# Weight products of 256 columns in place of 512 in a two-layer decoder trunk

## The chip, the core and the metric

The kernel runs on one core of one Trainium2 chip. The metric is the device time of one execution in microseconds (us), as the median of several executions. The profiled execution, from which every row below comes, is one execution taken by the hardware profiler. Engines are named as in the profile: PE is the matmul side of TensorE and PEld its weight loads, DVE is VectorE, ACT is ScalarE, POOL is GpSimd, SP issues DMAs.

## The reference

256 tokens of width 2048 pass through two residual layers. The first mixes tokens with a gated MLP, the second with an attention whose keys, values and forget gates come from the residual stream after the first layer. Each is followed by a convolutional feed-forward of width 5632. All products of tokens with a weight matrix are fp32.

```python
def reference(x, ...):
    h = x
    # layer 0
    z = gelu(rmsnorm(h, a_norm) @ a_w_in); u, v = split(z)
    h = h + (u * (W_s @ rmsnorm(v) + b_s)) @ a_w_out
    h = h + conv_ffn(rmsnorm(h, f_norm[0]), ...)
    k, v, c = fox_shared_kv(h, kv_norm, w_kvf, b_f, k_norm)
    # layer 1
    q, g = split(rmsnorm(h, b_norm) @ b_w_qg)
    h = h + (forgetting_attention(q, k, v, c) * sigmoid(g)) @ b_w_out
    h = h + conv_ffn(rmsnorm(h, f_norm[1]), ...)
    return rmsnorm(h, final_norm)

def conv_ffn(xn, w_up, conv_w, conv_b, w_down):
    h = xn @ w_up                      # 2048 -> 2 * 5632
    h = causal depthwise conv (width 3) of h, plus conv_b
    gate, val = split(h)
    return (silu(gate) * val) @ w_down # 5632 -> 2048
```

## The kernel before

**Weights.** Every weight matrix is laid out on the host in chunks of 128 partitions x 1024 fp32, 512 KB each, and read once. `Stream` is the planner of the whole program: a list of 785 chunks in a fixed order (the first one in two pieces, which makes 786 loads), all loaded by SP's queue. In step i of `Stream.run` it issues the load of chunk i+6 (into `raw`, four buffers), has chunk i+3 split in two by ACT and DVE (L82 and L83: `whi`, the weight rounded to the fp32r format, and `wlo`, the remainder; four buffers each), and issues the matmuls of chunk i on PE. After each chunk, `advance` lets every pending generator (the evictions and what follows them) run to its next `yield`, so that this work stands in the engines' queues between the chunks.

**Operands.** The tokens too are held in two parts: in an operand tile (`X1`, `ffn_H`, `mlp_X2`, `att_X2`) every feature row kt has 512 columns, of which the first 256 (`:T`, T = 256 tokens) are the rounded value and the last 256 (`T:`) the remainder. A product is the sum of three: weight high x token high, weight high x token low, weight low x token high.

**Feature-major tiles** (`feat_block`) make two output tiles of 128 features x 256 tokens in one PSUM buffer `ps` (128 x 2 x 512 fp32, m = 0, 1, each 512 wide half is one bank; three buffers). The weight is the stationary operand, the tokens stream past it. For each of four rows j and both m, one product with `whi` streams all 512 columns, so the two token parts land side by side in `ps[:, m, :T]` and `ps[:, m, T:]`; one product with `wlo` streams the first 256 and adds to `ps[:, m, :T]`. A chunk is 8 matmuls of 512 and 8 of 256 columns. 656 chunks are of this kind: `up` 352, `down` 176, and 32 each in `a_in_u`, `a_out`, `b_g` and `b_out`. The two side-by-side halves are added at eviction: `scaled_sum` (L299 to L301: ACT copies the second half into `half`, DVE adds it, DVE multiplies with the token scale `rB`), `residual` and `final` (two adds from PSUM to the residual stream `h`).

**The last tile of the program** (`last_block`, `down` of layer 1, p = 7, 11 chunks) is written otherwise: for each m, four `wlo` products, four `whi` products with the second token half and four with the first, all of 256 columns and all into `ps[:, m, :T]`. Its eviction (`final_tile`) follows each m in the last chunk.

**Token-major tiles** (`tok_block`) make 256 tokens x 512 features. Here the tokens are stationary and the weight chunk streams: for each of two rows and two token blocks tb three matmuls of 512 columns (token high x `whi`, token high x `wlo`, token low x `whi`), 12 to a chunk. 128 chunks are of this kind (`a_in_v`, `b_q`, `kvf_k`, `kvf_v`, 32 each). One small chunk, `kvf_f`, is handled by `forget`.

All weight matmuls go through `mm` (L166), which is why they share that line in the profile; the tiles tell them apart.

Of the kernel before, what the change touches and what calls it, by code (L numbers as in the profile page):

```python
# [10 lines left out]
F32 = mybir.dt.float32  # L11
F32R = mybir.dt.float32r
I32 = mybir.dt.int32
AF = mybir.ActivationFunctionType
# [118 lines left out]
def build(ctx, tc, d, out):  # L133
# [31 lines left out]
    def mm(o, a, b, start, stop):  # L165
        nc.tensor.matmul(o, a, b, start=start, stop=stop, skip_group_check=True)  # L166

    def feat_block(src, x, K, done, last=None):


        if last:
            return last_block(src, x, K, done, last)
        box = {}
        n = K // 4
        for c in range(n):
            def mult(hi, lo, c=c):
                if c == 0:
                    box["ps"] = main_ps()
                ps, xx = box["ps"], x()
                parts = (hi, lo) if c < n - 1 else (lo, hi)  # L180
                for i, part in enumerate(parts):
                    for j in range(4):
                        kt = 4 * c + j
                        for m in range(2):
                            w = part[:, j * 256 + m * P:j * 256 + (m + 1) * P]
                            if part is hi:
                                mm(ps[:, m, :], w, xx[:, kt, :], kt == 0, kt == K - 1)
                            else:
                                mm(ps[:, m, :T], w, xx[:, kt, :T], False, False)
                if c == n - 1:  # L190
                    s.start(done(ps))
            s.chunk(src[c], mult)

    def last_block(src, x, K, done, last):
        box = {}
        n = K // 4
        for c in range(n):
            def mult(hi, lo, c=c):
                if c == 0:
                    box["ps"] = main_ps()  # L200
                ps, xx = box["ps"], x()
                for m in range(2):
                    for part, half in ((lo, 0), (hi, 1), (hi, 0)):
                        for j in range(4):
                            kt = 4 * c + j
                            mm(ps[:, m, :T], part[:, j * 256 + m * P:j * 256 + (m + 1) * P],
                               xx[:, kt, half * T:(half + 1) * T], part is lo and kt == 0,
                               half == 0 and part is hi and kt == K - 1)
                    if c == n - 1:
                        last(ps, m)  # L210
                if c == n - 1:
                    s.start(done(ps))
            s.chunk(src[c], mult)

    def tok_block(src, x, done, load=None, prep=None):

        box = {}
        cuts = [(c, 0, 2) for c in range(8)]
        if prep:
            cuts[:1] = [(0, 0, 1), (0, 1, 1)]  # L220
        for c, j0, nj in cuts:
            def mult(hi, lo, c=c, j0=j0, nj=nj):
                kt0 = 2 * c + j0
                if kt0 == 0:
                    box["ps"] = main_ps()
                ps, xx = box["ps"], x()
                for j in range(nj):
                    kt = kt0 + j
                    w = slice(j * 512, (j + 1) * 512)
# [63 lines left out]
            for i in range(2):  # L293
                nc.vector.tensor_tensor(acc, acc, sq[:, i, :], op=OP.add)

    def scaled_sum(ps, a):

        t = small.tile([P, 2, T], F32, name="half", tag="half", bufs=2)
        nc.scalar.activation(t, ps[:, :, T:], AF.Copy)  # L299
        nc.vector.tensor_tensor(a, ps[:, :, :T], t, op=OP.add)  # L300
        nc.vector.tensor_tensor(a, a, rB[:, None, :].to_broadcast([P, 2, T]), op=OP.mult)  # L301

    def residual(p, gain):

        def done(ps):
# [25 lines left out]

    def final(p, gain):

        def done(ps):
            kts = (2 * p, 2 * p + 1)
            if p < 7:
                sq = small.tile([P, 2, T], F32, name="sq", tag="sq", bufs=2)
                for m, kt in enumerate(kts):
                    nc.vector.tensor_tensor(h[:, kt, :], h[:, kt, :], ps[:, m, :T], op=OP.add)
                    nc.vector.tensor_tensor(h[:, kt, :], h[:, kt, :], ps[:, m, T:], op=OP.add)  # L340
                    nc.scalar.activation(sq[:, m, :], h[:, kt, :], AF.Square)
                if p == 0:
                    nc.vector.tensor_tensor(acc, sq[:, 0, :], sq[:, 1, :], op=OP.add)
                else:
                    for i in range(2):
                        nc.vector.tensor_tensor(acc, acc, sq[:, i, :], op=OP.add)
            for kt in kts:
                nc.scalar.activation(h[:, kt, :], h[:, kt, :], AF.Copy, scale=column(gain + kt))
            if p == 5:
                nc.scalar.activation(warm, ones, AF.Sqrt)  # L350
            if p == 7:
                for m in range(2):
                    sum_tokens(tail["sums"], tail["sq"][:, m, :], False, m == 1)
                v = small.tile([P, 2], F32, name="ts_v", tag="ts_v", bufs=2)
                nc.vector.tensor_scalar(v, tail["sums"][:, :2], 1.0 / D, EPS, op0=OP.mult, op1=OP.add)
                t = small.tile([P, 2], F32, name="rs_t", tag="rs_t2", bufs=2)
                nc.scalar.activation(t, v, AF.Sqrt)
                nc.vector.reciprocal(rcol, t)
                newton(rcol, v, t)
                mp = token_rows()  # L360
                for a, b in ((0, 2), (2, 6), (6, 11), (11, 16)):
                    nc.vector.tensor_tensor(h[:, a:b, :], h[:, a:b, :],  # L362
                                            mp[:, None, :T].to_broadcast([P, b - a, T]), op=OP.mult)
                    nc.sync.dma_start(out[:, a:b, :], h[:, a:b, :])
            yield
        return done
# [66 lines left out]
        return done  # L433

    def u_done(p):
        def done(ps):
            X2, vt, wT, bB, _ = mlp_kept()
            u = ph.temp("u", [P, 2, T])
            scaled_sum(ps, u)
            yield  # L440
            nc.scalar.activation(u, u, AF.Gelu)
            mp = misc_ps()
# [20 lines left out]
        return ph.keep("H", [P, KF, 2 * T], F32R)  # L463

    def up_done(l, i):
        def done(ps):
            state["layer"] = l
            H = ffn_h()
            a = ph.temp("a", [P, 2, T])
            scaled_sum(ps, a)  # L470
            yield
            c = ph.temp("c", [P, 2, T])
            for m in range(2):
# [14 lines left out]

    def ffn(l, done):
        for i in range(KF):  # L490
            feat_block(d[f"up{l}"][4 * i:4 * i + 4], lambda: X1, KD, up_done(l, i))
        for p in range(8):
            feat_block(d[f"down{l}"][11 * p:11 * p + 11], ffn_h, KF, done(p), final_tile if l and p == 7 else None)


    def att(key):
# [155 lines left out]
            yield  # L652

    def g_done(p):
        def done(ps):
            X2, o = att("X2"), att("q")
            gg = ph.temp("big", [P, 512], bufs=6).rearrange("p (a b) -> p a b", a=2)
            scaled_sum(ps, gg)
            yield
            while state["done"] < NH or state["gates"] < p:  # L660
                yield
# [112 lines left out]
```

## Time and profile before

| What | Value |
|---|---|
| Time, median of 3 executions | 2244.74 us (2244.12 to 2244.78) |
| The profiled execution's own time | 2244.26 us |
| Its span, first to last instruction | 2242.6 us |
| Matmul records, weight-load records | 12546, 12546 |
| Weight bytes and inputs read from HBM | 417.88 MB |
| ACT busy, DVE busy | 1193.5 us, 1528.5 us |
| Mean granted TensorE clock | 0.998 |

How to read it: the span is what the profiler saw, and 1.7 us of the execution's own time lie around it. Matmuls are pipelined, and their ends in the profile are modelled, so the busy time of one matmul overlaps the next; what a matmul costs in a stream is the distance between starts, which the timeline shows for groups of equal matmuls. A weight load (PEld) is recorded for each matmul and overlaps with the matmul ahead of it.

### The profile page before, as it was taken

The page shows a single profiled execution, that of the slowest core. Times are in us where ns is not written, and L with a number is a line of the kernel's source. Part 1 is how long each engine was busy: PE and PEld are TensorE (multiplying, and loading weights), DVE is VectorE, ACT ScalarE, POOL GpSimd, SP SyncE. Part 2 cuts the span into 40 slices and gives each one's busy share as a digit, 9 for nine tenths or more (in the row PEclk, how much of TensorE's full clock was granted, in tenths as well). Part 3 has the DMA queues.
Part 4 walks back from the last instruction along what each step waited for, and adds up shares of the span by engine and source line. Part 5 has one row for each costly group of instructions (what it writes and reads, how often), then busy time and mean ns, then how long its engine had stood idle before and what let it go on. Part 6 is the DMA issues. An engine that isn't in the chain of part 4 may idle for free.

```text
span 2242.6 us, 32429 instructions
## 1 busy us (share of the span) xinstructions
PE 2228.1 (99%) x12546; PEld 1927.1 (86%) x12546; DVE 1528.5 (68%) x2219; ACT 1193.5 (53%) x1625; POOL 19.2 (1%) x41
## 2 busy tenths in 40 slices
PE   9999999999999999999999999999999999999998
PEld 7888888888888888888788888888888888888887
DVE  6566777777777755557786567677777777765554
ACT  6544455555555544445444666446555555544442
POOL 0000000000000000000000110000000000000000
PEclk9999999999999999999999999999999999999999
DMA  8555555656555555555555555555555555565553
GB/s 299 180 187 173 191 190 191 192 190 189 193 191 188 190 183 191 197 190 177 171 183 188 166 168 179 187 189 193 191 188 188 191 191 191 190 196 188 191 190 127
DMA packets 116443, 422.12 MB, mean 188 GB/s; under 512 B 13232, under 2 KB 13376, under 8 KB 116032
## 3 DMA queue, kind: packets, MB, share of 16 engines
q1 hardware_dynamic: 115344, 417.93, 56.7%
q0 software_dynamic: 768, 2.10, 0.3%
q8 instruction: 98, 1.61, 0.3%
q14 instruction: 57, 0.47, 0.1%
q10 hardware_dynamic: 176, 0.02, 0.0%
HBM read 417.88 MB, written 2.11 MB: 187 GB/s over the span
## 4 chain that ended last, share of the span: by engine, by line
PE 99%; DVE 0%; DMA 0%; ACT 0%; SPq 0%; DVEq 0%; issue 0%
PE ps L166 97%; PE mp L446 0%; PE mp L530 0%; PE mp L616 0%; DMA raw<-a_in_v 0%; PE mp L631 0%; PE mp L639 0%; PE mp L640 0%; PE mp L615 0%; PE mp L638 0%; DVE h L362 0%; PE mp L329 0%; PE mp L277 0%; DVE wlo L83 0%; DVEq L768 0%; ACT whi L82 0%
## 5 line engine op out<-in xcount | busy, mean ns | idle before, releaser
L83 DVE TENSOR_TENSOR wlo<-raw,whi 128x1024 fp32r<-128x1024 f32 (+1 forms) x786 | 953.3, 1221 | 378.8 <-ACT whi L82 377.3
L82 ACT ACTIVATE whi<-raw 128x1024 fp32r<-128x1024 f32 (+1 forms) x786 | 822.1, 1054 | 383.2 <-PE ps L166 353.9
L166 PE MATMUL ps<-X,whi 128*128 128x512 f32 x3328 | 829.6, 396 | 0.0
L166 PEld LDWEIGHTS ps<-X,whi 128*128 128x128 f32 x3328 | 602.7, 188 | 120.4
L166 PEld LDWEIGHTS ps<-X,wlo 128*128 128x128 f32 x3328 | 426.2, 188 | 28.1
L166 PE MATMUL ps<-X,wlo 128*128 128x256 f32 x3328 | 430.7, 277 | 0.0
L166 PE MATMUL ps<-ffn_H,whi 128*128 128x512 f32 (+1 forms) x1496 | 355.4, 381 | 0.0
L166 PEld LDWEIGHTS ps<-ffn_H,whi 128*128 128x128 f32 x1496 | 258.7, 188 | 45.3
L299 ACT ACTIVATE half<-ps 128x512 f32<-128x512 f32 x104 | 62.1, 597 | 256.1 <-PE ps L166 256.1
L166 PEld LDWEIGHTS ps<-ffn_H,wlo 128*128 128x128 f32 x1408 | 184.6, 188 | 13.8 <-DVE h L324 0.3
L166 PE MATMUL ps<-ffn_H,wlo 128*128 128x256 f32 x1408 | 188.5, 277 | 0.2 <-DVE h L324 0.2
L300 DVE TENSOR_TENSOR ffn_a<-ps,half 128x512 f32<-128x512 f32 x88 | 60.9, 692 | 175.1 <-ACT half L299 175.1
L166 PE MATMUL ps<-whi,att_X 128*128 128x512 f32 x512 | 168.1, 400 | 0.0
L480 DVE SCALAR_TENSOR_TENSOR ffn_c<-ffn_a,col,ffn_c 128x255 f32<-128x255 f32 x352 | 162.1, 481 | 6.3
L166 PE MATMUL ps<-whi,X 128*128 128x512 f32 x512 | 162.8, 395 | 0.9 <-ACT whi L82 0.9
L476 ACT ACTIVATE ffn_c<-ffn_a,col 128x256 f32<-128x256 f32 x176 | 96.4, 595 | 47.3 <-DVE ffn_a L301 47.3
L166 PEld LDWEIGHTS ps<-whi,X 128*128 128x128 f32 x512 | 96.2, 188 | 21.9 <-ACT whi L82 1.5
L166 PEld LDWEIGHTS ps<-whi,att_X 128*128 128x128 f32 x512 | 96.3, 188 | 20.4
L166 PE MATMUL ps<-wlo,X 128*128 128x512 f32 x256 | 99.7, 390 | 1.0 <-DVE wlo L83 1.0
L166 PE MATMUL ps<-wlo,att_X 128*128 128x512 f32 x256 | 100.0, 391 | 0.0
L245 ACT ACTIVATE X<-h,col 128x256 fp32r<-128x256 f32 x64 | 29.0, 500 | 101.8 <-DVE h L308 99.5
L250 ACT ACTIVATE ffn_H<-ffn_c 128x256 fp32r<-128x256 f32 x88 | 36.7, 418 | 70.2 <-DVE ffn_c L484 70.2
(147 smaller groups left out, 1215.0 us busy)
## 6 DMA issues: line engine op xcount, KB each, us to landing
raw<-up SPq DMA_DIRECT2D x352, 512.0 KB, 3.8
raw<-down SPq DMA_DIRECT2D x176, 512.0 KB, 4.2
raw<-a_in_u SPq DMA_DIRECT2D x32, 512.0 KB, 3.6
raw<-a_out SPq DMA_DIRECT2D x32, 512.0 KB, 4.3
raw<-b_q SPq DMA_DIRECT2D x32, 512.0 KB, 4.2
raw<-kvf_k SPq DMA_DIRECT2D x32, 512.0 KB, 4.0
raw<-kvf_v SPq DMA_DIRECT2D x32, 512.0 KB, 3.6
raw<-b_g SPq DMA_DIRECT2D x32, 512.0 KB, 3.3
```

The source lines that it names most:

```text
L82: self.nc.scalar.activation(hi[:, :n], raw, AF.Copy)
L83: self.nc.vector.tensor_tensor(lo[:, :n], raw, hi[:, :n].bitcast(F32), op=OP.subtract)
L166: nc.tensor.matmul(o, a, b, start=start, stop=stop, skip_group_check=True)
L245: nc.scalar.activation(dst[:, kt, :T], h[:, kt, :], AF.Copy, scale=g)
L250: nc.scalar.activation(dst[..., :T], src, AF.Copy)
L299: nc.scalar.activation(t, ps[:, :, T:], AF.Copy)
L300: nc.vector.tensor_tensor(a, ps[:, :, :T], t, op=OP.add)
L476: nc.scalar.activation(c[:, m, :], a[:, m, :], AF.Identity, scale=w[2], bias=column(C_CONVB + l * 2 * KF + f))
L480: nc.vector.scalar_tensor_tensor(c[:, m, n:], a[:, m, :T - n], w[k], c[:, m, n:], op0=OP.mult, op1=OP.add)
```

## The change

It has three parts. Line numbers of the code after the change are a few lower than before from `tok_block` on.

1. **Feature-major tiles.** A product of `whi` with 512 token columns becomes two products with the same stationary weight, one per token half, and both add to `ps[:, m, :T]`, where the `wlo` product adds too. A chunk is then 24 matmuls of 256 columns. An argument `wide` names chunks that keep the 512-column product: 66 of 656 (all of `b_g`, 32; one chunk of each `a_in_u` tile, 8; one chunk each in `a_out` and `b_out`; in each layer, the four chunks of the first `up` tile, one chunk of each of six further ones, and one chunk each of two `down` tiles). `last_block` is gone; its tile uses the same code, with m outermost in the last chunk alone. In every chunk the `whi` products now come first; before, the last chunk of a tile had `wlo` first.
2. **Evictions.** A tile without a wide chunk has nothing in `ps[:, m, T:]`. The ACT copy and one DVE add are left out there; `scaled_sum` becomes `scaled`, which multiplies from PSUM. `final` handles both rows of a tile in one instruction.
3. **Token-major tiles.** Each matmul of 512 weight columns becomes two of 256 columns with the same stationary tokens, into the two halves of the same bank.

The products and the sums are the same; the number of weight matmuls in the program goes from 12 152 to 18 320 (6168 more), and a weight load goes with each.

```diff
-    def feat_block(src, x, K, done, last=None):
-        if last:
-            return last_block(src, x, K, done, last)
+    def feat_block(src, x, K, done, wide=(), tile_done=None):
...
-                parts = (hi, lo) if c < n - 1 else (lo, hi)
-                for i, part in enumerate(parts):
+                def product(part, half, j, m):
+                    kt = 4 * c + j
+                    w = part[:, j * 256 + m * P:j * 256 + (m + 1) * P]
+                    first = kt == 0 and part is hi and half in (None, 0)
+                    last = kt == K - 1 and part is lo
+                    if half is None:
+                        mm(ps[:, m, :], w, xx[:, kt, :], first, False)
+                    else:
+                        mm(ps[:, m, :T], w, xx[:, kt, half * T:(half + 1) * T], first, last)
+                halves = (None,) if c in wide else (0, 1)
+                if tile_done and c == n - 1:
+                    for m in range(2):
+                        for j in range(4):
+                            for half in halves:
+                                product(hi, half, j, m)
+                        for j in range(4):
+                            product(lo, 0, j, m)
+                        tile_done(ps, m)
+                else:
                     for j in range(4):
-                        kt = 4 * c + j
                         for m in range(2):
-                            w = part[:, j * 256 + m * P:j * 256 + (m + 1) * P]
-                            if part is hi:
-                                mm(ps[:, m, :], w, xx[:, kt, :], kt == 0, kt == K - 1)
-                            else:
-                                mm(ps[:, m, :T], w, xx[:, kt, :T], False, False)
+                            for half in halves:
+                                product(hi, half, j, m)
+                    for j in range(4):
+                        for m in range(2):
+                            product(lo, 0, j, m)
                 if c == n - 1:
-                    s.start(done(ps))
+                    s.start(done(ps, bool(wide)))
...
-                        mm(ps[:, tb, :], a, hi[:, w], kt == 0, False)
-                        mm(ps[:, tb, :], a, lo[:, w], False, False)
-                        mm(ps[:, tb, :], b, hi[:, w], False, kt == KD - 1)
+                        for i, (st, mv) in enumerate(((a, hi), (a, lo), (b, hi))):
+                            for q in range(2):
+                                mm(ps[:, tb, q * T:(q + 1) * T], st, mv[:, j * 512 + q * T:j * 512 + (q + 1) * T],
+                                   kt == 0 and i == 0 and q == 0, kt == KD - 1 and i == 2)
...
-    def scaled_sum(ps, a):
-        t = small.tile([P, 2, T], F32, name="half", tag="half", bufs=2)
-        nc.scalar.activation(t, ps[:, :, T:], AF.Copy)
-        nc.vector.tensor_tensor(a, ps[:, :, :T], t, op=OP.add)
-        nc.vector.tensor_tensor(a, a, rB[:, None, :].to_broadcast([P, 2, T]), op=OP.mult)
+    def scaled(ps, both, a):
+        src = ps[:, :, :T]
+        if both:
+            nc.scalar.activation(a, ps[:, :, T:], AF.Copy)
+            nc.vector.tensor_tensor(a, ps[:, :, :T], a, op=OP.add)
+            src = a
+        nc.vector.tensor_tensor(a, src, rB[:, None, :].to_broadcast([P, 2, T]), op=OP.mult)
...
-            nc.vector.tensor_tensor(hh, hh, ps[:, :, T:], op=OP.add)
+            if both:
+                nc.vector.tensor_tensor(hh, hh, ps[:, :, T:], op=OP.add)
...
-            feat_block(d[f"up{l}"][4 * i:4 * i + 4], lambda: X1, KD, up_done(l, i))
+            feat_block(d[f"up{l}"][4 * i:4 * i + 4], lambda: X1, KD, up_done(l, i),
+                       range(4) if i == 0 else (0,) if i % 8 == 1 else ())
-            feat_block(d[f"down{l}"][11 * p:11 * p + 11], ffn_h, KF, done(p), final_tile if l and p == 7 else None)
+            feat_block(d[f"down{l}"][11 * p:11 * p + 11], ffn_h, KF, done(p), (0,) if p % 4 == 0 else (),
+                       final_tile if l and p == 7 else None)
...
-        feat_block(d["a_in_u"][4 * p:4 * p + 4], lambda: X1, KD, u_done(p))
+        feat_block(d["a_in_u"][4 * p:4 * p + 4], lambda: X1, KD, u_done(p), (1,) if p else (0,))
-        feat_block(d["a_out"][4 * p:4 * p + 4], mlp_x2, KD, residual(p, C_FNORM))
+        feat_block(d["a_out"][4 * p:4 * p + 4], mlp_x2, KD, residual(p, C_FNORM), () if p else (1,))
-        feat_block(d["b_g"][4 * p:4 * p + 4], lambda: X1, KD, g_done(p))
+        feat_block(d["b_g"][4 * p:4 * p + 4], lambda: X1, KD, g_done(p), range(4))
-        feat_block(d["b_out"][4 * p:4 * p + 4], lambda: att("X2"), KD, residual(p, C_FNORM + KD))
+        feat_block(d["b_out"][4 * p:4 * p + 4], lambda: att("X2"), KD, residual(p, C_FNORM + KD), () if p else (0,))
```

PE's instructions in the `up` stage of layer 0, from the second tile on (`X_73` is `X1`; of the two names behind the arrow the first is streamed and the second stationary; the size is that of the output). Before:

```order
L277 MATMUL mp<-ident,rcol 128x128 x2
L166 MATMUL ps<-X_73,whi 128x512 x8
L166 MATMUL ps<-X_73,wlo 128x256 x8
L166 MATMUL ps<-X_73,whi 128x512 x8
L166 MATMUL ps<-X_73,wlo 128x256 x8
L166 MATMUL ps<-X_73,whi 128x512 x8
```

With the change:

```order
L273 MATMUL mp<-ident,rcol 128x128 x2
L166 MATMUL ps<-X_73,whi 128x512 x8
L166 MATMUL ps<-X_73,wlo 128x256 x8
L166 MATMUL ps<-X_73,whi 128x256 x16
L166 MATMUL ps<-X_73,wlo 128x256 x8
L166 MATMUL ps<-X_73,whi 128x256 x16
```

The second tile's first chunk is one of those that stay wide; from its second chunk on, eight `whi` matmuls of 512 columns have become sixteen of 256, while the `wlo` rows stay as they were.

PE's instructions at the end of the program, in the last chunk of the last tile, where PE waits for DVE's add to `h` between the two m. Before:

```order
L166 MATMUL ps<-ffn_H,wlo 128x256 x4
L166 MATMUL ps<-ffn_H,whi 128x256 x8
L329 MATMUL mp<-ones,acc 128x1 x2
L166 MATMUL ps<-ffn_H,wlo 128x256 x4
L166 MATMUL ps<-ffn_H,whi 128x256 x8
L329 MATMUL mp<-ones,sq 128x1 x4
```

With the change:

```order
L166 MATMUL ps<-ffn_H,whi 128x256 x8
L166 MATMUL ps<-ffn_H,wlo 128x256 x4
L328 MATMUL mp<-ones,acc 128x1 x2
L166 MATMUL ps<-ffn_H,whi 128x256 x8
L166 MATMUL ps<-ffn_H,wlo 128x256 x4
L328 MATMUL mp<-ones,sq 128x1 x4
```

The counts and the place of the two sums are the same; `whi` and `wlo` have changed places.

More of the change, by code (lines that the diff above doesn't have):

```diff
@@ L184, in mult @@
                         for m in range(2):
-                            w = part[:, j * 256 + m * P:j * 256 + (m + 1) * P]
-                            if part is hi:
-                                mm(ps[:, m, :], w, xx[:, kt, :], kt == 0, kt == K - 1)
-                            else:
-                                mm(ps[:, m, :T], w, xx[:, kt, :T], False, False)
-                if c == n - 1:
-                    s.start(done(ps))
[L192 to L212, printed above, removed]
@@ L228, in mult @@
                     kt = kt0 + j
-                    w = slice(j * 512, (j + 1) * 512)
                     for tb in range(2):
@@ L332, in final, with done @@
     def final(p, gain):
-        def done(ps):
+        def done(ps, both):
             kts = (2 * p, 2 * p + 1)
             if p < 7:
[L337 to L346, printed above, removed]
+                hh = h[:, 2 * p:2 * p + 2, :]
+                nc.vector.tensor_tensor(hh, hh, ps[:, :, :T], op=OP.add)
+                if both:
+                    nc.vector.tensor_tensor(hh, hh, ps[:, :, T:], op=OP.add)
+                square_into_acc(p)
             for kt in kts:
@@ L435, in u_done, with done @@
     def u_done(p):
-        def done(ps):
+        def done(ps, both):
             X2, vt, wT, bB, _ = mlp_kept()
             u = ph.temp("u", [P, 2, T])
-            scaled_sum(ps, u)
+            scaled(ps, both, u)
             yield
@@ L465, in up_done, with done @@
     def up_done(l, i):
-        def done(ps):
+        def done(ps, both):
             state["layer"] = l
@@ L469, in done @@
             a = ph.temp("a", [P, 2, T])
-            scaled_sum(ps, a)
+            scaled(ps, both, a)
             yield
@@ L654, in g_done, with done @@
     def g_done(p):
-        def done(ps):
+        def done(ps, both):
             X2, o = att("X2"), att("q")
             gg = ph.temp("big", [P, 512], bufs=6).rearrange("p (a b) -> p a b", a=2)
-            scaled_sum(ps, gg)
+            scaled(ps, both, gg)
             yield
```

2 lines of the change are left out of this document (1 added, 1 removed).

## Prediction

> **What bounds the kernel now.** I read the busy shares first, then the chain of waits, then the starts of the matmuls.
>
> ```profile
> PE 2228.1 (99%) x12546; PEld 1927.1 (86%) x12546; DVE 1528.5 (68%) x2219; ACT 1193.5 (53%) x1625; POOL 19.2 (1%) x41
> PEclk9999999999999999999999999999999999999999
> PE 99%; DVE 0%; DMA 0%; ACT 0%; SPq 0%; DVEq 0%; issue 0%
> PE ps L166 97%; PE mp L446 0%; PE mp L530 0%; PE mp L616 0%; DMA raw<-a_in_v 0%; PE mp L631 0%; PE mp L639 0%; PE mp L640 0%; PE mp L615 0%; PE mp L638 0%; DVE h L362 0%; PE mp L329 0%; PE mp L277 0%; DVE wlo L83 0%; DVEq L768 0%; ACT whi L82 0%
> ACT whi L82 <- PE ps L166: 353.9, 286, 2.2
> ```
>
> The chain that ended last is PE for 99% of the span, and the weight products of L166 for 97%. The other engines wait for PE, not the reverse: ACT's split of the weights idles 353.9 us in all because PE has not given a buffer back. So a chunk costs what PE needs for it, and time is won or lost only by the distance between matmul starts, and at the two ends. The clock row says that no slice was throttled.
>
> What a chunk costs is read best from long stretches of the chain and from the start times of the groups.
>
> ```profile
> 293.61 726.57 PE ps L166 x4184
> 1020.19 0.34 PE mp L329 x4
> 1043.30 8.26 PE ps L166 x36
> 295.32 1.07 PE L166 MATMUL ps<-X,wlo 128*128 128x256 f32 x8
> 296.23 2.02 PE L166 MATMUL ps<-X,whi 128*128 128x512 f32 x8
> 298.09 1.07 PE L166 MATMUL ps<-X,wlo 128*128 128x256 f32 x8
> 299.00 2.02 PE L166 MATMUL ps<-X,whi 128*128 128x512 f32 x8
> ```
>
> The first row is 260 feature-major chunks (4160 matmuls) and 2 token-major ones (24). The third row is 3 token-major chunks: 8.26 / 3 = 2.753 us. So a feature-major chunk in its present form costs (726.58 - 2 x 2.753) / 260 = 2.773 us. The start times divide it: eight `whi` products take 298.09 - 296.23 = 1.86 us, 232 ns each; eight `wlo` products 0.91 us, 114 ns each. A product of 512 columns costs more than two of 256. That is the whole matter of this case.
>
> The new form has run in this program already, in its last tile:
>
> ```profile
> 2199.82 1.07 PE L166 MATMUL ps<-ffn_H,whi 128*128 128x256 f32 x8
> 2200.73 0.62 PE L166 MATMUL ps<-ffn_H,wlo 128*128 128x256 f32 x4
> ...
> 2225.66 1.07 PE L166 MATMUL ps<-ffn_H,whi 128*128 128x256 f32 x8
> 2227.93 0.50 PE L329 MATMUL mp<-ones,acc 128*128 128x1 f32 x4
> ```
>
> Between the first row and the third lie 19 periods of 12 matmuls of 256 columns: 25.84 / 19 = 1.360 us, or 113.3 ns a matmul, `whi` and `wlo` alike, each with a weight load of its own. 24 of them are 2.720 us.
>
> **The change part by part.** *Feature-major tiles.* 656 chunks less the 11 of the last tile, which had the new form before, less 66 that stay wide, are 579. Each goes from 2.773 to 2.720 us: 0.0534 us, or 6.7 ns for each of its eight split products. 579 x 0.0534 = 30.9 us.
>
> *Token-major tiles.* 128 chunks go from 2.753 to 2.720 us if their 24 matmuls run at the same 113.3 ns: 128 x 0.033 = 4.2 us. No row shows a streamed weight of 256 columns. The bounds are 2.753 (two halves cost what the whole did) and 2.720; I take the latter, since what streams is the same number of columns of the same type.
>
> *What the pairs add.* New is that two neighbouring matmuls have the same stationary operand, which is loaded anew for each. The trace has loads with every matmul:
>
> ```profile
> 2199.40:2226.50 27.10, 27.10 (x241) 27.10 (x240) 12.07 (x14) 9.92 (x12) 0.00 (x0) 1.00 0.29 98
> 294.00:790.00 496.00, 496.00 (x2864) 432.12 (x2863) 375.35 (x531) 293.28 (x402) 0.00 (x0) 1.00 0.59 190
> L166 PEld LDWEIGHTS ps<-X,whi 128*128 128x128 f32 x3328 | 602.7, 188 | 120.4
> ```
>
> The columns are the stretch, its length, then busy time of PE, PEld, DVE, ACT and POOL, granted clock, DMA share and GB/s. In the last tile PEld is busy all 27.10 us of 27.10, against 432 of 496 in `up`. So in the new form loads stand back to back and there is no slack left for them. They keep the pace of 113.3 ns there with DMA at 98 GB/s; with the changed kernel they must do so at 190 GB/s. The nearest row for that is the `wlo` group of the `up` stage, at 190 GB/s: 0.91 / 8 = 113.8 ns, and this group stands behind 512-column products. I take 113.3; with 113.8 a chunk would be 2.730 us and the gain 579 x 0.043 + 128 x 0.023 = 27.8 us, which is the weak bound. Nothing in the trace runs 256 columns of this type faster, so the strong bound is the sum itself, with some 3 us for the rounding of rows (10 ns in 1.86 us is 0.5%, and the long stretches hold that down).
>
> *Evictions.* Left out are the ACT copy and one DVE add of the tiles without a wide chunk; in `up` that is 74 of 88.
>
> ```profile
> L299 ACT ACTIVATE half<-ps 128x512 f32<-128x512 f32 x104 | 62.1, 597 | 256.1 <-PE ps L166 256.1
> L300 DVE TENSOR_TENSOR ffn_a<-ps,half 128x512 f32<-128x512 f32 x88 | 60.9, 692 | 175.1 <-ACT half L299 175.1
> L83 DVE TENSOR_TENSOR wlo<-raw,whi 128x1024 fp32r<-128x1024 f32 (+1 forms) x786 | 953.3, 1221 | 378.8 <-ACT whi L82 377.3
> ```
>
> ACT loses 74 x 0.597 = 44 us and DVE 74 x 0.692 = 51 us of work. I cost it at nothing, because PE's 2.7 us a chunk cover both engines: DVE's share in `up` is 375.35 of 496. DVE's multiply now waits for PE itself instead of for ACT's copy. Behind it in DVE's queue stands the split (L83) of a chunk that PE takes three steps, some 8 us, later, so that wait reaches nobody. Even if the cover were gone, this part could only help.
>
> *Order and ends.* In the last chunk of a tile `whi` now precedes `wlo`; both were split three chunks ahead. The start up to the first `wlo` wait is set by DMA, ACT and DVE. The tail behind the last products is a chain of small steps, 2242.6 - 2228.13 = 14.5 us, and has the same 12 matmuls between the two adds.
>
> ```profile
> 11.14 0.50 PE L166 MATMUL ps<-wlo,X 128*128 128x512 f32 x1 [0.76 <-DVE wlo L83]
> 2228.13 0.43 DVE h L324
> ```
>
> I count both ends as unchanged.
>
> *Sum.* 30.9 + 4.2 = 35.1 us off the profiled execution's 2244.26 us (1.7 us of which lie around its span of 2242.6): 2209.2. The median lies 0.5 us above that execution, so I forecast 2209.5 us.
>
> **The rivals.** *The surplus stays with the pair* (4 in 100). If the 6.7 ns belong to a `whi` product that meets both token halves, and not to the width of 512, the two halves of a pair would carry it on. Then nothing is gained, and the time is about 2244 us. For it: the surplus is seen on such products alone. Against it: the token-major rows have 512 columns and other operands and show 2.753 / 12 = 229.4 ns, 2.8 above two halves; and in the last tile `whi` meets both halves at 113.3.
>
> *The second load of the same weights is exposed* (5 in 100), the case that ends slower. In the last tile a weight comes back only after four other matmuls. If a load of the operand that is in use had to wait until the matmul ahead ends, a part of its 188 ns would show: at most 188 - 113.3 = 75 ns on each of 6168 pairs, 463 us and a time of 2707; it decides from 35.1 / 6168 = 5.7 ns a pair on, and at a third of the load's length past its cover, 25 ns, the time would be 2209 + 154 = 2363 us. Against it: in the token-major chunks two of three matmuls in a row have the same stationary tokens, and their 229.4 ns show no such step, though 512 columns would cover it.
> The Trainium skill's page "Perfetto Trace Analysis", section "Identifying the Most-Contended Engine", judges TensorE's headroom by the share of weight loads and not by that of matmuls; by it the kernel goes from 86% to nearly full, and this rival's ground is where it would first show.
>
> *A fixed price for every matmul* (1 in 100). If each start cost something beside its columns, 6168 more of them would cost and not gain. The rows leave little room: taking 10 ns of rounding against the change, a `wlo` product is 0.92 / 8 = 115 ns, and two of them are 0.6 ns over the 229.4 of a token-major product; on all pairs that is 3.7 us, a time of 2248 us. It would need the last tile's 113.3 to be an exception.
> The Trainium skill has this rule on the page "TensorE: Matmul & The Clock Gate", section "Back-to-back issue gap": N columns take N / 2.4 ns plus 2.5 ns, so a split adds 2.5 ns, an estimated 15.4 us over all splits and a time near 2260 us. The trace disagrees on the sign: 232 ns for 512 columns, 2 x 113.3 for the halves.
>
> *Half gain* (5 in 100): the loads lose 0.5 ns to 1 ns a matmul to DMA traffic. With 24 x 1 ns a chunk, 707 chunks lose 17 us, and the time is 2226 us.
>
> *Another engine becomes the bound* (1 in 100). DVE needs 375.35 / 179 = 2.10 us a chunk in `up` before the adds go, and the DMA rate rises by 2% on 190 GB/s. Neither is near 2.72 us; the time would be between.
>
> **How the numbers follow.** The forecast of 2209.5 us has 84 in 100. Its own range is 2205 to 2217, from the strong bound and the 27.8 us of the weak one. Half of the half-gain case lies within a few us of that end, so I set 2204 to 2218; what is left out is the rivals. About 0.2%, 4.5 us, is what a measurement of this kernel tells from no change. Faster by more than that: the forecast, the half gain and the last rival, 90 in 100. Within it: the surplus that stays and the fixed price, 5. Slower: the exposed load, 5.
>
> **What would show it.** Right: `whi` groups of 16 at 113.3 ns from start to start, sixteen of them in 1.81 us where eight wide ones took 1.86; PEld near 100% of the `up` stage; feature chunks at 2.720 and the wide ones still at 2.77; token chunks at 2.72; the tail still 14.5 us. Wrong in the first step: starts within a pair at 113 and between pairs at 120 or more (the surplus stays), or the second load of a pair starting late with PE idle ahead of it (the slower rival). Wrong in the cover: PE waiting for DVE or ACT inside `up`.

## The result and the profile after

The changed kernel takes 2225.39 us (median of 4 executions, 2222.26 to 2228.70), the kernel before 2244.51 us on the same chip. The ratio is 0.9915, 95% interval 0.9898 to 0.9932. It is faster, but by 19 us where 35 were forecast, and the time lies outside the range of 2204 to 2218. Its executions also differ by 6.4 us, those of the kernel before by 0.7 us.

The profiled execution took 2226.94 us with a span of 2225.2 us. Its busy shares, clock and chain, from the page:

```profile
PE 2211.2 (99%) x18714; PEld 2182.7 (98%) x18714; DVE 1467.6 (66%) x2106; ACT 1151.3 (52%) x1544; POOL 19.0 (1%) x41
PEclk9999999999999999999999999999999999999999
PE 99%; DMA 0%; DVE 0%; ACT 0%; SPq 0%; DVEq 0%; issue 0%
```

And ACT's largest wait, from the view of waits (us in total, times, longest):

```profile
ACT whi L82 <- PE ps L166: 631.8, 439, 2.2
```

PE is still the whole chain, and ACT waits for it longer than before. The loads (PEld) went from 86% to 98% of the span, the granted clock is full. So no other engine took over, and the missing 16 us lie inside the stream of matmuls. The view of matmuls in time shows where. First the `up` stage of layer 0, then `a_out`; columns are start, length of the group, engine, line, operation, tiles, shape and count:

```profile
303.47 1.98 PE L166 MATMUL ps<-X,whi 128*128 128x256 f32 x16
305.28 1.07 PE L166 MATMUL ps<-X,wlo 128*128 128x256 f32 x8
306.19 1.98 PE L166 MATMUL ps<-X,whi 128*128 128x256 f32 x16
...
204.19 2.05 PE L166 MATMUL ps<-mlp_X,whi 128*128 128x256 f32 x16
206.07 1.10 PE L166 MATMUL ps<-mlp_X,wlo 128*128 128x256 f32 x8
207.01 2.05 PE L166 MATMUL ps<-mlp_X,whi 128*128 128x256 f32 x16
```

In `up` 24 matmuls take 306.19 - 303.47 = 2.72 us, as forecast. In `a_out` the same 24 take 2.82 us, and both groups are longer: `whi` 1.88 / 16 = 117.5 ns, `wlo` 0.94 / 8 = 117.5 ns. There are two distances, and they do not mix. The chain gives them over long stretches (start, length, engine, line, count; the first row holds 3 wide chunks, the second 8 and two token-major ones):

```profile
198.71 93.17 PE ps L166 x768
298.13 713.08 PE ps L166 x6224
...
1017.53 16.97 PE ps L166 x144
1034.49 0.44 PE mp L526 x4
1034.93 8.17 PE ps L166 x72
1043.10 0.44 PE mp L526 x4
1043.53 14.14 PE ps L166 x120
```

With the wide chunks at 2.773 us taken out, the first row is at (93.17 - 3 x 2.773) / 720 = 117.8 ns a matmul. The token-major pieces between two groups of small products (L526, the transposes) are 16.97 / 144 = 117.8 ns, then 8.17 / 72 = 113.5, then 14.14 / 120 = 117.8, with the same code in each. Inside a piece, from the fourth matmul on, the distances are 112 to 115 ns or 116 to 120 ns, never of both kinds. A straight line through the starts of the long runs gives 113.33 ns (15 runs of 752 or more) and 117.78 ns (the run of 728 at 200.4 us); I call these the short and the long distance. They differ by 4.44 ns.

I counted the 256-column matmuls in stretches of 12 or more with the long distance: 3912 of 17 440, in the first 55 us, in `a_in_u`, in `a_out` and in most of the token-major pieces. 3912 x 4.44 ns = 17.4 us. Without them the span would be 2225.2 - 17.4 = 2207.8 us; the forecast, as a span, was 2242.6 - 35.1 = 2207.5 us. So the long distance is the whole error of the profiled execution, to 0.3 us.

Is it DMA traffic? Busy times in equal stretches of `a_out` and `up` (columns as in the prediction; the count behind PE is the matmuls in 83 us):

```profile
202.00:285.00 83.00, 83.00 (x707) 83.00 (x707) 53.34 (x66) 39.26 (x51) 0.00 (x0) 1.00 0.58 190
302.00:385.00 83.00, 83.00 (x735) 83.00 (x734) 61.07 (x87) 47.47 (x64) 0.00 (x0) 1.00 0.65 197
```

The slower stretch has the lower DMA rate, and DVE and ACT do less in it. The clock is 1.00 in both. But the rate follows the pace, since every chunk brings its 512 KB: the rows show that no extra traffic goes with the long distance, and no more. What settles it is the run with four small products below.

The tail is as forecast: 2225.2 - 2210.63 = 14.6 us.

```profile
2210.63 0.43 DVE h L323
2211.10 1.67 PE ps L166 x12
```

### The profile page after: what moved, and what is told of

Its sections match the earlier page's. It is cut to its first block, busy times and chain, and to the rows that moved or that the text cites. A ratio compares the mean times of both kernels' runs of the same rounds, so it can differ in the third digit from the quotient of the medians.

```text
span 2225.2 us, 44638 instructions
## 1 busy us (share of the span) xinstructions
PE 2211.2 (99%) x18714; PEld 2182.7 (98%) x18714; DVE 1467.6 (66%) x2106; ACT 1151.3 (52%) x1544; POOL 19.0 (1%) x41
## 4 chain that ended last, share of the span: by engine, by line
PE 99%; DMA 0%; DVE 0%; ACT 0%; SPq 0%; DVEq 0%; issue 0%
PE ps L166 97%; PE mp L440 0%; PE mp L526 0%; PE mp L612 0%; DMA raw<-a_in_v 0%; PE mp L627 0%; PE mp L635 0%; PE mp L636 0%; PE mp L611 0%; PE mp L634 0%; DVE h L356 0%; PE mp L328 0%; PE mp L273 0%; DVE wlo L83 0%; DVEq L764 0%; ACT whi L82 0%
## 5 line engine op out<-in xcount | busy, mean ns | idle before, releaser
L166 PE MATMUL ps<-X,whi 128*128 128x256 f32 (+1 forms) x6176 | 829.8, 286 | 0.0
L166 PEld LDWEIGHTS ps<-X,whi 128*128 128x128 f32 x6176 | 760.0, 188 | 16.3
L166 PE MATMUL ps<-ffn_H,whi 128*128 128x256 f32 (+1 forms) x2784 | 348.4, 278 | 0.2 <-DVE h L323 0.2
L166 PEld LDWEIGHTS ps<-ffn_H,whi 128*128 128x128 f32 x2784 | 330.5, 188 | 1.3 <-DVE h L323 0.3
L166 PE MATMUL ps<-whi,att_X 128*128 128x256 f32 x1024 | 170.6, 283 | 0.0
L166 PE MATMUL ps<-whi,X 128*128 128x256 f32 x1024 | 164.5, 280 | 0.7 <-ACT whi L82 0.7
L166 PE MATMUL ps<-wlo,X 128*128 128x256 f32 x512 | 101.6, 280 | 0.8 <-DVE wlo L83 0.8
L166 PE MATMUL ps<-wlo,att_X 128*128 128x256 f32 x512 | 101.5, 279 | 0.0
L166 PEld LDWEIGHTS ps<-wlo,X 128*128 128x128 f32 x512 | 78.1, 188 | 1.2 <-DVE wlo L83 1.2
L166 PEld LDWEIGHTS ps<-wlo,att_X 128*128 128x128 f32 x512 | 78.2, 188 | 0.0
```

## The experiments

The theory after this reading, called "kept cadence" below: a stream of 256-column products runs at 113.33 or 117.78 ns; which of them is settled where the stream begins behind other products, and nothing inside the stream changes it. The rivals: DMA traffic slows the loads; or the long distance belongs to the code and operands of certain stages.

**One part at a time.** The token-major part undone:

```diff
-                        for i, (st, mv) in enumerate(((a, hi), (a, lo), (b, hi))):
-                            for q in range(2):
-                                mm(ps[:, tb, q * T:(q + 1) * T], st, ...
+                        mm(ps[:, tb, :], a, hi[:, w], kt == 0, False)
+                        mm(ps[:, tb, :], a, lo[:, w], False, False)
+                        mm(ps[:, tb, :], b, hi[:, w], False, kt == KD - 1)
```

> The token-major part is undone (512 columns there again), the feature-major part stays. Theory (kept cadence): a stream of 256-column products runs at one of two distances, 113.33 or 117.78 ns, which is drawn where it begins behind other products and is kept to its end; products of 512 columns do not keep it. Then token-major chunks cost about 2.753 us in every stage, against a mix of 2.72 and 2.827 us before, some 6 us less in all: 2219 us (2215 to 2223). Rival 1 (DMA traffic slows the loads): token-major chunks of 512 columns were slowed as well, so their cost varies with the DMA rate from stage to stage; 2223 to 2226 us. Rival 2 (the form: a pair of loads of the same tokens is dear): the same 2219 us, and the a_in_u and a_out stages stay at 117.8 ns.

Measured: 2215.40 us (2213.70 to 2215.88), ratio 0.9869, interval 0.9854 to 0.9884. It beats the changed kernel, at the lower end of the range expected. From the chain of its profiled execution:

```profile
196.32 89.94 PE ps L166 x768
1028.75 8.26 PE ps L166 x36
```

The token-major pieces are back at 8.26 / 3 = 2.753 us a chunk, in every stage. The surprise is the first row: the same 768 matmuls of `a_out` and the head of `up` that took 93.17 us take 89.94 us, and nothing in their code was touched. What stands ahead of `a_in_u` is different, and the whole stretch from there on has the short distance. That speaks against the third theory, which had named these stages as slow in themselves.

The kernel before with the token-major part alone:

> The kernel before with the token-major part of the change alone. Kept cadence: the stages split at the small products (L526-like transposes, sums); each piece is at 113.3 or at 117.8 ns throughout; all fast 2240 us, all slow 2254 us, a mix like that of the changed kernel 2250 us, slower than before. Rival 1: 2240 to 2245 us with distances that vary within a piece. Rival 2: all pieces at 117.8 ns, 2254 us.

Measured: 2252.93 us (2251.68 to 2253.04), ratio 1.0036, interval 1.0024 to 1.0049: slower than before, as a mix of both distances must be. 2600 of its 5448 narrow token-major and `wlo` matmuls in runs of 12 or more have the long distance; 2600 x 4.44 ns = 11.6 us, against 4.2 us to be gained, so 7.4 us slower; measured are 8.7 (interval 5.4 to 11.0). This part of the change loses.

**No wide chunk at all.** All six `wide` arguments are left empty.

```diff
-                       range(4) if i == 0 else (0,) if i % 8 == 1 else ())
+                       ())
...
-        feat_block(d["a_in_u"][4 * p:4 * p + 4], lambda: X1, KD, u_done(p), (1,) if p else (0,))
+        feat_block(d["a_in_u"][4 * p:4 * p + 4], lambda: X1, KD, u_done(p), ())
```

> No chunk keeps the wide form. Kept cadence: each up and down stage (264 chunks) has no break after its first three chunks and holds one distance to its end; a layer is then 28 us longer at 117.8 than at 113.3 ns, so the time is near 2222 us with both fast, 2250 with one slow and 2278 with both slow, and it can differ by such steps from execution to execution. Rival 1: 2222 us (66 chunks save 0.053 us each). Rival 2 (a wide chunk in each tile makes a_in_u slow): a_in_u at 113.3 ns, 2218 us.

Measured: 2281.68 us (2279.41 to 2282.09), ratio 1.0164, interval 1.0150 to 1.0178. 66 chunks were made narrow, each of which would save 0.05 us by the forecast's reckoning, and the kernel became 56 us slower than with them. Its chain, layer 0:

```profile
294.18 5.76 PE ps L166 x48
300.16 740.59 PE ps L166 x6288
1040.75 0.34 PE mp L328 x4
```

740.59 / 6288 = 117.78 ns: 740 us without a break at the long distance, from the start of the second `up` tile to the end of `down` and two token-major chunks; layer 1 the same. The changed kernel had 713.08 us there, for 64 matmuls fewer. The stretch of `up` that was shown above of the changed kernel is here:

```profile
302.00:385.00 83.00, 83.00 (x707) 83.00 (x706) 58.88 (x84) 45.62 (x62) 0.00 (x0) 1.00 0.61 185
```

707 matmuls in 83 us against 735, at 185 GB/s against 197. Of the three expectations only kept cadence had this case, with 2278 us.

**Small products as breaks.** No wide chunk in `up` and `down`, and behind up tile i stand i mod 5 fp32 products into a buffer that nobody reads (the profile records each of them as two matmuls):

```diff
+            if i % 5:
+                mp = misc_ps()
+                for _ in range(i % 5):
+                    if l:
+                        nc.tensor.matmul(mp[:, :P], ident, ident, start=True, stop=True)
+                    else:
+                        nc.tensor.matmul(mp[:, :1], ident, ones[:, :1], start=True, stop=True)
             scaled(ps, both, a)
```

> No wide chunk in up and down; behind each up tile i stand i mod 5 extra small fp32 products into an unread buffer, of 1 column in layer 0 and of 128 columns in layer 1 (88 tiles, 176 of them in all; nothing of the result changes). Kept cadence: the distance changes at these places alone and is constant between them; some tiles at 113.3, some at 117.8 ns. Rivals 1 and 2: every up tile stays at 113.3 ns as in the changed kernel. Time is not the point; about 0.2 to 0.4 us for each place.

Measured: 2262.50 us in one execution. In layer 0, where the products have one column, the stage begins at 117.8 ns; behind the first small product, at 304.39 us, it is at 113.3, and all 67 later breaks of this kind, in both layers, leave it there. In layer 1, where they have 128, the first break (one product) left the long distance, the second (two) ended it. So a break can change the distance, and where these added products changed it they ended the long one, never the short one. That "some tiles" would be long among them was wrong: the draw is not even.

That suggests a sharp test: the kernel without wide chunks, and four instructions more.

```diff
+            if i in (1, 2):
+                mp = misc_ps()
+                nc.tensor.matmul(mp[:, :1], ident, ones[:, :1], start=True, stop=True)
             scaled(ps, both, a)
```

> The kernel without any wide chunk (2281.7 us, both up and down stages at 117.78 ns throughout) with four instructions more: one product of one column into an unread buffer behind the up tiles 1 and 2 of each layer. Kept cadence: behind one of the two the stream falls to 113.33 ns and stays there to the end of down, so some 255 of 264 chunks of each layer get 0.107 us less: 2 x 27 = 54 us, 2228 us (one layer alone: 2255 us). Rivals (DMA traffic; the code or operands of a stage): four instructions change nothing, 2282 us.

Measured: 2223.16 us (2219.90 to 2226.76), ratio 0.9901, interval 0.9884 to 0.9917. Four products of one column took 58 us off a kernel of 2281.7 us. Matmuls in time around the first of them:

```profile
304.35 2.05 PE L166 MATMUL ps<-X,whi 128*128 128x256 f32 x16
306.24 1.10 PE L166 MATMUL ps<-X,wlo 128*128 128x256 f32 x8
307.18 2.05 PE L166 MATMUL ps<-X,whi 128*128 128x256 f32 x16
309.06 1.11 PE L166 MATMUL ps<-X,wlo 128*128 128x256 f32 x8
310.01 0.28 PE L466 MATMUL mp<-ones,ident 128*128 128x1 f32 x2
310.15 2.08 PE L166 MATMUL ps<-X,whi 128*128 128x256 f32 x16
312.06 1.07 PE L166 MATMUL ps<-X,wlo 128*128 128x256 f32 x8
312.97 1.98 PE L166 MATMUL ps<-X,whi 128*128 128x256 f32 x16
314.78 1.07 PE L166 MATMUL ps<-X,wlo 128*128 128x256 f32 x8
```

And the chain of that layer from there on:

```profile
310.28 11.01 PE ps L166 x96
321.41 691.01 PE ps L166 x6096
```

The last `whi` groups ahead of the small product take 1.88 us (309.06 - 307.18), the second one behind it 1.81 (314.78 - 312.97), and the 691.01 us that follow are at 691.01 / 6096 = 113.35 ns. The same operands, the same code, the same stage: one small instruction separates them. Layer 1 did the same at its first small product. In the profiled executions 54.7 of the 55.3 us between the two spans are the matmuls that left the long distance (12 309 x 4.44 ns). Both rivals fall here.

**Two small products in the changed kernel.** One behind each of the first two `a_in_u` tiles.

> The changed kernel with two instructions more: behind the first and the second a_in_u tile a product of one column into an unread buffer. Kept cadence: in the run of 256-column products behind them a_in_u and a_out go from 117.78 to 113.33 ns and stay there up to the up stage, 60 chunks by 0.107 us, 6 us less: 2219 us (2217 to 2223), and the token-major stages keep their mix. Rival 2 (a_in_u's and a_out's code or operands are slow in themselves): no change, 2225 us, and 117.8 ns in these stages. Rival 1 (DMA traffic): no change.

Measured: 2221.73 us (2221.13 to 2222.18), ratio 0.9899, interval 0.9882 to 0.9915. The number is near, but the test failed: in the profiled execution `a_in_u` had the short distance already ahead of the first added product, so that these could show nothing, while a long stretch had come to lie in the token-major stage ahead (the run that begins at 60.3 us in the changed kernel, at 113.33 ns, and at 59.6 us here, at 117.78). The edit stands behind that run: the first 880 matmuls of the two programs are the same. So the code up to a break does not fix the distance behind it.

**Fewer wide chunks.** Token-major products of 512 columns, and of the 66 wide chunks 41 are kept: one at the head of `a_in_u`, the first `up` tile of each layer, all of `b_g`.

> Token-major chunks of 512 columns as in the run with that part undone, and 25 of the 66 wide chunks made narrow (left: one at the head of a_in_u, the first up tile of each layer, all of b_g). Kept cadence: without breaks the up and down stages hold 113.33 ns over 260 chunks, so these 25 wide chunks were insurance alone: 25 x 0.053 = 1.3 us less, 2214 us (2213 to 2216). If the wide chunks are needed again and again, up and down fall to 117.78 ns somewhere: each 100 chunks so lost cost 10.7 us, up to 2270 us.

Measured: 2212.09 us (2211.91 to 2213.99), ratio 0.9859, interval 0.9844 to 0.9873, the best of the study. Its chain has the short distance throughout:

```profile
290.14 712.72 PE ps L166 x6264
1489.86 705.88 PE ps L166 x6228
```

705.88 / 6228 = 113.34 ns over 700 us without a break (the first row holds two token-major chunks of 512 columns besides). The 25 chunks were insurance. The gain over the first experiment, 3.3 us against 1.3 expected, is within what the two intervals leave.

**The distance by itself.** Behind 16 `up` tiles of layer 1 stand 64 products of the same fp32r type into an unread buffer, with other numbers of streamed and stationary columns:

```diff
+            if l and 2 <= i < 18:
+                n, cols = [(256, 128), (320, 128), (384, 128), (512, 128), (256, 64), (256, 32), (320, 64),
+                           (512, 64)][(i - 2) % 8]
+                mp = misc_ps()
+                for r in range(64):
+                    mm(mp[:cols, :n], X1[:, r % KD, r % 2 * P:r % 2 * P + cols], X1[:, (r + 1) % KD, :n], r == 0, r == 63)
```

> As the run with the token-major part undone, and behind 16 up tiles of layer 1 a stream of 64 products of the same type into an unread buffer: by turns 256, 320, 384 and 512 columns with 128 stationary columns, 256 with 64 and with 32, 320 and 512 with 64; each twice. If the weight load sets the distance of the 256-column products and the two cadences, then with half the stationary columns 256 columns run well under 113 ns (about 107) and in one cadence, and 320 columns at 128 stationary are near 5/4 of 107 with no second value. If the streamed columns set it, fewer stationary columns change nothing: 113.3 ns, and 320 columns take 141.7 ns.

Measured: 4163.36 us in one execution, with a mean granted clock of 0.659. The clock record begins only at 973 us, far ahead of the added products, and stands at 0.56 from there to the end; the page counts the time before as 1.00. But PE was slow from the start. Two chunks of 256-column products, from before and after that point:

```profile
300.72 3.94 PE L166 MATMUL ps<-X,whi 128*128 128x256 f32 x16
306.28 4.04 PE L166 MATMUL ps<-X,whi 128*128 128x256 f32 x16
...
1201.94 3.19 PE L166 MATMUL ps<-X,whi 128*128 128x256 f32 x16
1206.49 3.28 PE L166 MATMUL ps<-X,whi 128*128 128x256 f32 x16
```

A chunk of 24 takes 5.56 us at 300 us and 4.55 us at 1202 us, against 2.72 in the first experiment. Nothing of the distances can be read from this run, so it ran once more:

> The stream of 64 products behind 16 up tiles of layer 1 once more, since the granted clock fell to 0.56 in the middle of its first run. If the weight load sets the distance of the 256-column products and the two cadences, then with 64 or 32 stationary columns 256 streamed columns run at about 107 ns, and 320 columns at 128 stationary at about 5/4 of that, 133 ns. If the streamed columns set it, fewer stationary columns change nothing: 113.3 ns, and 320 columns take 141.7 ns.

Measured: 2378.79 us, clock 0.998. The groups in time; in the shape the number behind the asterisk is that of the stationary columns:

```profile
1512.77 7.84 PE L166 MATMUL mp<-X 128*128 128x256 f32 x64
1531.76 9.55 PE L166 MATMUL mp<-X 128*128 128x320 f32 x64
1552.04 11.26 PE L166 MATMUL mp<-X 128*128 128x384 f32 x64
1574.45 14.69 PE L166 MATMUL mp<-X 128*128 128x512 f32 x64
1600.28 7.42 PE L166 MATMUL mp<-X 128*64 128x256 f32 x64
1618.42 7.42 PE L166 MATMUL mp<-X 128*32 128x256 f32 x64
1636.55 9.54 PE L166 MATMUL mp<-X 128*64 128x320 f32 x64
1656.88 14.88 PE L166 MATMUL mp<-X 128*64 128x512 f32 x64
```

Less the length of the last matmul (0.28 us at 256 columns, 0.31 at 320, 0.33 at 384, 0.39 at 512) and over 63 distances these are 120.0, 146.7, 173.4 and 227.0 ns with 128 stationary columns, 113.3 with 64 and with 32, 146.5 at 320 columns with 64 (0.01 us a row is 0.2 ns), and 230 at 512 with 64. Both expectations are half right. 113.3 ns is not set by the number of stationary columns: with 64 and with 32 it is the same, so it goes with the 256 streamed columns. With 128 stationary columns 6.7 ns come on top in this stream. I put them down to the load, but fewer stationary columns also mean fewer output rows, and the run does not separate the two; at 512 columns the smaller load is even the slower one, 230 against 227. At 320 columns 128 and 64 stationary columns cost the same.

## Why the prediction was wrong, step by step

**What bounds the kernel: right.** PE is 99% of the chain after as before, and the ends are unchanged (14.6 us behind the last products, 14.5 before).

**The price of two halves against a whole: right where the short distance holds.** The `up` stage has 2.72 us a chunk where 2.773 stood. The sum of 35.1 us is met to 0.3 us once the long distance is taken off, and the run with few wide chunks, short throughout, lies within the forecast's range with 2212.09 us. At that distance splitting is cheaper than not splitting, and the rival of a fixed price for every matmul is out, as is that of the surplus that stays with the pair.

**The step that failed** is "What the pairs add", at the words "I take 113.3; with 113.8 a chunk would be 2.730 us". One price was taken for all narrow matmuls, from a last tile and a `wlo` group that both showed the short distance, and the bound beside it came from rounding in a row. In its place the runs show two prices, 113.33 and 117.78 ns, 2.72 and 2.827 us a chunk. The second is dearer than the chunk of 512-column products that the change removes (2.773), so a narrow chunk gains 0.053 us or loses 0.054. The token-major term was hit hardest: "two halves cost what the whole did" was called the far bound, and the part costs 8.7 us by itself (2252.93 against 2244.21 us). The step itself had the sentence that leads there: "loads stand back to back and there is no slack left for them". I went on as if a row at that limit were a row with a margin.

The second price stood in the profile of before. The last chunk of a tile has sixteen `wlo` products in a row there. The first two rows are the end of `down` of layer 0, the last two the first `up` tile of that layer, behind the small sums (L329) and one group of `whi`:

```profile
1010.84 1.98 PE L166 MATMUL ps<-ffn_H,wlo 128*128 128x256 f32 x16
1012.66 2.02 PE L166 MATMUL ps<-ffn_H,whi 128*128 128x512 f32 x8
...
289.48 2.05 PE L166 MATMUL ps<-X,wlo 128*128 128x256 f32 x16
291.36 2.03 PE L166 MATMUL ps<-X,whi 128*128 128x512 f32 x8
```

The first sixteen take 1.82 us, 113.8 ns each, the others 1.88 us, 117.5 ns each, and the first `up` tile of layer 1 (at 1504.83 us) has 1.88 as well. At 117.5 ns a chunk is 2.82 us: with this row as the far bound the range would have reached beyond the time of before.

**The half-gain rival had the time by luck, and not the cause.** 2226 us was its price, at 5 in 100, by DMA traffic that takes 0.5 to 1 ns from each load. Four small products undo the loss in the same stage.

**The second load of the same weights** is out in the form it was given: `wlo` products, whose weights stand alone, have the long distance too (0.94 / 8). That a surplus could show once loads stand back to back was right in kind. (Of its two times 2707 us counts from 2244 and 2363 us from 2209; from 2209 the first is 2672. And in the last tile a weight comes back after three other matmuls, not four.)

**Evictions, order of `whi` and `wlo`, other engines: right.** ACT's busy time fell by 42.2 us and DVE's by 60.9 with no effect on the chain.

**The wide chunks** were the part I left unasked: 66 chunks that pay 0.05 us each. Without them the kernel is slower than before by 1.6%. They are breaks at which a stream can come back to the short distance: in `up` the four wide chunks at the head are needed or something like them, in `a_in_u`, one to a tile, the first led from the short to the long distance and the seven after it did not end it, and 25 others were not needed.

**What stays open.** That the distance is settled at a break and kept between breaks is shown. What at a break settles it is not. The kind of product counts. I counted the places where a small product alone stands between two narrow streams, in the six profiled executions that have them. The added products of one column ended the long distance at three of three places where it stood and left the short one at 38 of 38. The program's own sums (L328, two products of one column with another stationary operand) were followed by the long distance at 18 of 18, eight of them behind the short one. The transposes between token-major pieces (L526) led to the long one at 82 of 96. But the kind is not all: the two transposes (L273) at 60 us ended the long distance in the changed kernel and left it in the run with two small products, behind the same 880 matmuls. Eight products (L440) with a wide chunk behind them kept whichever distance stood before, eight times each. And the wide chunk at the head of `a_in_u` led from short to long in the changed kernel and from long to short in two other runs, so a wide chunk can also do harm.

A load that has no room beside 256 streamed columns, and that stays late once it is late, would be one account. It is not shown: at either distance a load starts some 3 ns behind the start of the matmul ahead. The 6.4 us between executions of the changed kernel fit draws that change (6.4 us is 1440 matmuls by 4.44 ns), and only one execution of it was profiled.

## What to carry to other kernels

A stream whose weight loads are busy all the time can have more than one steady pace, so its price is not read from one place: look for a second value among stretches of the same instruction, in the profile of before too, and for what stands at their borders. Where a change takes the last slack from a resource, the bound for the range is the slowest row of the same instruction, not the rounding of the best one. And code that looks like an odd exception (a form kept in 66 places) deserves a question of its own before its cost is summed up.

## What the hardware showed that was not expected

- Two paces of the same instruction, 113.33 and 117.78 ns, held for 706 and 741 us without a break, with a single product of one column able to end the longer one while the program's own sums were followed by it at 18 of 18 places; and 120.0 ns in a stream whose stationary and streamed operands come from one tile.
- 512 columns in one product take 229.4 ns in the token-major and 232 ns in the feature-major chunks of this kernel (227 in the added stream), two products of 256 columns 226.7 at the short distance and 235.6 at the long one: the narrow form is the cheaper one where it holds its pace.
- In one run PE took 5.56 us for a chunk that takes 2.72 elsewhere, at 300 us, and 4.55 us at 1202 us, where the granted clock was 0.56, as from 973 us to the end of the run. Ahead of 973 us the trace has no clock record, and the 1.00 of the page did not show the slow PE: the distances did. Up to the added products its code is that of the first experiment.
